# Gates, both projections and the merge of a hybrid decoder block computed with the tokens stationary in the array, and the merged result laid out by feature by way of DRAM

## The chip, the core and the metric

The kernel runs on one core of one Trainium2 chip. The metric is the device time of one execution in microseconds (us). A core has TensorE for matrix products (PE in the rows; PEld is its loading of the stationary operand), VectorE (DVE), ScalarE (ACT), GpSimd (POOL) and SyncE (SP), each with its own instruction queue that it works off in order, and 16 DMA engines that all queues share. Matrix products end in PSUM, of which VectorE and ScalarE take them away.

## The reference, cut to what matters

One decoder block with 256 tokens, a model width of 2048 and float32 throughout. The part that the change touches:

```python
u = rms_norm(h, g_mix[l])
proj = u @ w_in[l]
q, k, v, z, gb, gc, gate_a, gate_c = jnp.split(proj, split_points, axis=-1)
...
y_attn = sliding_window_attention(q, k, v, attn_sinks[l]) @ w_attn_proj[l]   # (256 x 1024) @ (1024 x 2048)
y_conv = short_gated_conv(z, gb, gc, conv_w[l]) @ w_conv_proj[l]             # (256 x 1024) @ (1024 x 2048)
merged = jax.nn.sigmoid(gate_a) * y_attn + jax.nn.sigmoid(gate_c) * y_conv
h = h + merged @ w_mix_out[l]                                               # (256 x 2048) @ (2048 x 2048)
```

gate_a and gate_c are the last two 2048 columns of proj. Cross-attention over 256 memory tokens and a SwiGLU feed-forward with 5632 hidden features follow.

## The kernel before, in words

Every weight matrix is read once from DRAM, in tiles of two times 128 rows by 512 columns (512 KB), issued on SP into five `raw` buffers (line 81). `split` (lines 56 and 57) makes two float32r halves of a tile: ScalarE rounds it to `whi`, VectorE subtracts to get `wlo`; three buffers each. The activations are kept split in the same way, as `X[:, k, 0]` (high) and `X[:, k, 1]` (low), with features on the partitions. A product is high*high + high*low + low*high.

There are two ways to run such a product over a chunk of 512 output columns:

- `gemm_ft` (lines 85 to 111) holds a 128x128 block of the weight in the array and streams tokens. For each block there is a matmul of 512 columns (high weight against high and low tokens, side by side, line 97) and one of 256 columns (low weight against high tokens, line 101). The result has features on the partitions and fills four PSUM banks; ScalarE copies the right half out (line 108) and VectorE adds the left half (line 142). The rest of the work on a result is held back in `pending` and run among the next chunk's weight tiles.
- `gemm_tf` (lines 113 to 139) holds a 128x128 block of tokens in the array and streams 512 columns of the weight: three matmuls of 512 columns (lines 123, 124, 125) for each of two token blocks. The result has tokens on the partitions and fills two PSUM banks.

The order of the work is that of the code, rearranged by a scheduler at build time that places each engine's instructions; `hooks` attach small pieces of work to a weight tile (to the index k0 of its first 128 rows) of a running product. The stages that matter here, all with `gemm_ft` in the kernel before:

- the gates: eight chunks of 512 columns with 16 row tiles each. `evac_g` adds, scales by the norm factor laid along the tokens (`r0[1]`) and applies the sigmoid into `sa` (attention) or `sc` (convolution). The attention itself (scores, probabilities, values) is hooked into these chunks;
- the projections: four times a chunk of w_attn_proj (8 row tiles, `evac_a`) and a chunk of w_conv_proj (8 row tiles, `evac_m`). `evac_m` merges and splits straight into `MG`, which w_mix_out reads. Loads, sums and transposes of the memory tokens are hooked into these chunks (`mem_hooks`: `mst`, `mnat`, `XM`);
- w_mix_out: four chunks with 16 row tiles, `gemm_tf`, residual add into `h` (line 592). Each finished chunk of `h` is laid out by feature by way of DRAM: `bounce` writes it to the DRAM tile `hd` and reads it back in four pieces into `hst` (lines 227 and 232), on SP's queue; `feat` then lets VectorE transpose blocks of 32x32 (line 212).

## Time and profile before

| | us |
|---|---|
| median of 3 runs | 1450.93 |
| lowest and highest of them | 1450.8 and 1451.27 |
| the profiled execution | 1449.95 |
| its span, first to last instruction | 1448.2 |
| granted TensorE clock over the span, of full speed | 0.997 |

The profile is of one execution. Its rows give the span's times from the first instruction on; the profiled execution's own time is 1.75 us above the span. Busy times of PE are modelled at their ends, so distances between starts tell more than durations do.

### The profile page before, as it was taken

What the parts mean: (1) busy time and instruction counts of PE and PEld (TensorE: products, weight loads), DVE (VectorE), ACT (ScalarE), POOL (GpSimd) and SP (SyncE); (2) the same over time, 40 slices, a digit from 0 to 9 for tenths busy, and PEclk for the clock granted to TensorE, in tenths of its full rate; (3) what the DMA queues carried; (4) which work ended last, traced back from release to release, by engine and by line L of the source; (5) the groups of instructions that cost most, each with busy time, mean ns of one, the idle gap of its engine ahead of it and who ended that gap; (6) DMA issues with size and microseconds to landing.
All of it is one profiled execution on the core that took longest, in us unless ns stands there. A gap on an engine that the chain in (4) does not pass through costs nothing.

```text
span 1448.2 us, 20203 instructions
## 1 busy us (share of the span) xinstructions
PE 1431.6 (99%) x7712; PEld 1224.4 (85%) x7712; DVE 882.8 (61%) x1297; ACT 721.2 (50%) x1111; POOL 61.6 (4%) x90
## 2 busy tenths in 40 slices
PE   8999999999999999999999999999999999999997
PEld 7888888888888888899888888888888888888886
DVE  5458678565569875675665665655444556656554
ACT  6443645555456654556654544544333445445443
POOL 1081000010001000000000000000000000000000
PEclk9999999999999999999999999999999999999999
DMA  8655455576667677755666666666556666666663
GB/s 264 189 176 173 140 167 150 156 222 195 190 200 212 207 257 240 240 191 161 192 186 190 189 189 190 180 199 193 196 190 191 187 191 189 189 190 186 199 195 118
DMA packets 146496, 277.21 MB, mean 191 GB/s; under 512 B 9204, under 2 KB 18000, under 8 KB 146272
## 3 DMA queue, kind: packets, MB, share of 16 engines
q1 hardware_dynamic: 144192, 269.52, 60.9%
q0 software_dynamic: 2176, 6.40, 1.7%
q8 instruction: 60, 0.98, 0.3%
q14 instruction: 36, 0.29, 0.1%
q10 hardware_dynamic: 32, 0.01, 0.0%
HBM read 271.70 MB, written 4.19 MB: 191 GB/s over the span
## 4 chain that ended last, share of the span: by engine, by line
PE 95%; POOL 2%; DMA 1%; issue 1%; DVE 0%; ACT 0%; SPq 0%; ACTq 0%; POOLq 0%; DVEq 0%
PE acc L97 42%; PE acc L101 21%; PE acc L124 10%; PE acc L123 10%; PE acc L125 10%; PE sps L434 1%; PE ops L487 1%; DMA raw<-in_w_in 0%; PE tp L476 0%; POOL sa L339 0%; DMA hst<-hd 0%; DMA hd<-h 0%; POOL sa L342 0%; POOL sa L341 0%; POOL sa L340 0%
## 5 line engine op out<-in xcount | busy, mean ns | idle before, releaser
L57 DVE TENSOR_TENSOR wlo<-raw,whi 128x1024 fp32r<-128x1024 f32 (+1 forms) x506 | 608.3, 1207 | 522.3 <-ACT whi L56 522.1
L56 ACT CAST whi<-raw 128x1024 fp32r<-128x1024 f32 (+1 forms) x506 | 519.4, 1031 | 624.0 <-PE acc L97 353.4
L97 PE MATMUL acc<-X,whi 128*128 128x512 f32 x2368 | 805.0, 395 | 0.0
L101 PE MATMUL acc<-X,wlo 128*128 128x256 f32 x2368 | 607.3, 280 | 0.0
L97 PEld LDWEIGHTS acc<-X,whi 128*128 128x128 f32 x2368 | 435.3, 188 | 83.7 <-issue 0.8
L101 PEld LDWEIGHTS acc<-X,wlo 128*128 128x128 f32 x2368 | 445.5, 188 | 23.8 <-issue 0.8
L125 PE MATMUL acc<-whi,gT 128*128 128x512 f32 x352 | 136.9, 389 | 0.0
L124 PE MATMUL acc<-wlo,gT 128*128 128x512 f32 x352 | 136.9, 389 | 0.0
L123 PE MATMUL acc<-whi,gT 128*128 128x512 f32 x352 | 123.8, 389 | 0.0
L108 ACT COPY half<-acc 128x256 f32<-128x256 f32 x184 | 67.1, 369 | 22.4 <-PE acc L101 20.8
L123 PEld LDWEIGHTS acc<-whi,gT 128*128 128x128 f32 x352 | 66.1, 188 | 13.7
L125 PEld LDWEIGHTS acc<-whi,gT 128*128 128x128 f32 x352 | 66.0, 188 | 13.7
L124 PEld LDWEIGHTS acc<-wlo,gT 128*128 128x128 f32 x352 | 66.1, 188 | 13.7
L124 PE MATMUL acc<-wlo,MG 128*128 128x512 f32 x128 | 49.9, 390 | 0.4 <-DVE wlo L57 0.4
L125 PE MATMUL acc<-whi,MG 128*128 128x512 f32 x128 | 49.8, 389 | 0.0
L198 POOL TENSOR_TENSOR rstd<-ms,mhalf 128x2 f32<-128x2 f32 (+1 forms) x6 | 4.9, 810 | 947.2 <-DVE ms L196 947.2
L123 PE MATMUL acc<-whi,MG 128*128 128x512 f32 x128 | 44.9, 389 | 0.0
L97 PE MATMUL acc<-yc,whi 128*128 128x512 f32 x128 | 44.2, 397 | 0.2 <-DVE s L142 0.2
L97 PE MATMUL acc<-oT,whi 128*128 128x512 f32 x128 | 43.8, 396 | 0.0
L124 PE MATMUL acc<-wlo,X 128*128 128x512 f32 x96 | 37.6, 397 | 0.0
L123 PE MATMUL acc<-whi,X 128*128 128x512 f32 x96 | 34.6, 399 | 2.5 <-ACT X L221 2.5
L125 PE MATMUL acc<-whi,X 128*128 128x512 f32 x96 | 36.7, 393 | 0.0
(195 smaller groups left out, 1135.7 us busy)
## 6 DMA issues: line engine op xcount, KB each, us to landing
raw<-in_w_ffn_in SPq DMA_DIRECT2D x176, 512.0 KB, 4.4
raw<-in_w_in SPq DMA_DIRECT2D x134, 512.0 KB, 4.4
raw<-in_w_ffn_out SPq DMA_DIRECT2D x88, 512.0 KB, 4.6
raw<-in_w_mix_out SPq DMA_DIRECT2D x32, 512.0 KB, 5.7
raw<-in_w_attn_proj SPq DMA_DIRECT2D x16, 512.0 KB, 4.8
raw<-in_w_conv_proj SPq DMA_DIRECT2D x16, 512.0 KB, 5.1
raw<-in_w_xkv SPq DMA_DIRECT2D x8, 512.0 KB, 4.2
raw<-in_w_xkv SPq DMA_DIRECT2D x16, 256.0 KB, 2.7
```

The lines of the kernel that those rows point to most:

```text
L56: nc.scalar.copy(hi, src)
L57: nc.vector.tensor_tensor(out=lo, in0=src, in1=hi.bitcast(F32), op=ALU.subtract)
L97: nc.tensor.matmul(ps[m], lhsT=hi[:, k, ms], rhs=X[:, kk].rearrange("p s t -> p (s t)"), start=(kk == 0), stop=False,)
L101: nc.tensor.matmul(ps[m][:, :T], lhsT=lo[:, k, ms], rhs=X[:, kk, 0, :], start=False, stop=(kk == kt - 1),)
L108: nc.scalar.copy(t2, ps[m][:, T:])
L123: nc.tensor.matmul(o, lhsT=xh, rhs=hi[:, k, :cols], start=(kk == 0), stop=False)
L124: nc.tensor.matmul(o, lhsT=xh, rhs=lo[:, k, :cols], start=False, stop=False)
L125: nc.tensor.matmul(o, lhsT=xl, rhs=hi[:, k, :cols], start=False, stop=(kk == kt - 1))
L198: nc.gpsimd.tensor_tensor(out=r, in0=ms, in1=mhalf[:, :n], op=ALU.pow)
L434: nc.tensor.matmul(sps[par][:, j].rearrange("p a b -> p (a b)"), lhsT=qT[b:b + 64, hh // 2, t * P:(t + 1) * P], rhs=kT[b:b + 64, sw, kv // ...
L487: nc.tensor.matmul(ops[64 * par:64 * par + 64], lhsT=v_sb[:, kb, vs], rhs=pt[:, t + kb, par::2, :], start=(kb == 0), stop=(kb == t),)
```

## The change

The gates, both projections and the merge now run with `gemm_tf`: their results have tokens on the partitions, like those of w_mix_out. `evac_g` is one sigmoid on ScalarE out of PSUM, with the norm factor as its per-partition scale. `evac_a` is one product out of PSUM, `evac_m` a product out of PSUM and a sum. A finished chunk of the merge, in `sa`, is written to `hd` in DRAM and read back by feature, all on GpSimd's queue: for the first three chunks into the part of `sc` that is used up, for the last into a new tile `mg`. `mg_feat` (hooked to the next w_conv_proj chunk but one product later) and `mg_last` (hooked to row tiles 12 and 14 of w_mix_out's first chunk) let VectorE transpose it and split it into `MG`. w_mix_out's rows are read in the matching order.

```diff
--- before.py
+++ after.py
@@ -50,6 +50,7 @@
     tiny = ctx.enter_context(tc.tile_pool(name="tiny", bufs=4, side="right"))
     acc = ctx.enter_context(tc.tile_pool(name="acc", bufs=5, space=PSUM))
     tps = ctx.enter_context(tc.tile_pool(name="tps", bufs=3, space=PSUM))
+    dp = ctx.enter_context(tc.tile_pool(name="dp", bufs=2, space=bass.MemoryType.DRAM))
 
 
     def split(hi, lo, src):
@@ feat @@
@@ -212,7 +214,11 @@
             i = nc.vector.transpose(xt[:, k, :].rearrange("p (j b) -> p j b", b=Q), v[:, k0 + k, j0:j0 + nj, :])
             if late and not k:
                 tc.keep_in_program_order(i)
-        high_low([xt[:, k, :] for k in range(n)], kx, g, X, slice(j0 * Q, j0 * Q + nt))
+        tsl = slice(j0 * Q, j0 * Q + nt)
+        if g is None:
+            split(X[:, kx:kx + n, 0, tsl], X[:, kx:kx + n, 1, tsl], xt)
+        else:
+            high_low([xt[:, k, :] for k in range(n)], kx, g, X, tsl)
 
     def high_low(srcs, kx, g, X, tsl=slice(0, T)):
         for k, src in enumerate(srcs):
@@ -226,13 +232,18 @@
         v = src.rearrange("(j b) (i f) -> i b j f", b=Q, i=P // Q)
         eng.dma_start(stage[Q * i:Q * (i + 1), j0:j0 + nj, :], v[i][:, j0:j0 + nj, :])
 
-    def bounce(c, st, eng=nc.sync):
-
+    def bounce_out(src, eng):
         hd = dp.tile([T, C], F32, tag="hd", name="hd")
-        eng.dma_start(hd.rearrange("(t p) f -> p t f", p=P), h[:, :, c * C:(c + 1) * C])
+        eng.dma_start(hd.rearrange("(t p) f -> p t f", p=P), src)
+        return hd
+
+    def bounce_in(hd, st, eng):
         for i in range(P // Q):
             stage_in(st, hd, i, eng=eng)
 
+    def bounce(src, st, eng=nc.sync):
+
+        bounce_in(bounce_out(src, eng), st, eng)
     def spread(r, name):
 
         rB = const.tile([P, T], F32, tag="rB", name=name, bufs=2)
@@ rotary's scratch @@
-        sa = mp.tile([P, KD, T], F32, tag="sa", name="sa")
+        sa = mp.tile([P, D // C, NT, C], F32, tag="sa", name="sa")
 
 
         def rotary(s_sb, nh):
@@ -492,7 +503,7 @@
                 sl = slice(t * P, (t + 1) * P)
                 split(oT[:, 2 * g:2 * g + 2, 0, sl], oT[:, 2 * g:2 * g + 2, 1, sl], ops)
 
-        sc = mp.tile([P, KD, T], F32, tag="sc", name="sc")
+        sc = mp.tile([P, D // C, NT, C], F32, tag="sc", name="sc")
         steps = {
             0: [qk_T], 1: [lambda: scores(0)], 2: [lambda: probs_T(0), lambda: scores(1)],
             3: [lambda: values(0), lambda: probs_T(1), lambda: scores(2)],
@@ -540,33 +551,26 @@
                     hooks = {0: [lambda: do["stage"](0)], 2: [lambda: do["stage"](1)],
                              4: [lambda: do["nat"](0)], 6: [lambda: do["nat"](1)]}
 
-                def evac_g(m, p0, p1, c=c, dst=dst):
-                    o = dst[:, c * (C // P) + m, :]
-                    add(o, p0, p1)
-                    yield
-                    scale(o, r0[1])
-                    nc.scalar.activation(o, o, AF.Sigmoid)
-
-                gemm_ft(W, KD, X1, base + c * C, evac_g, hooks=hooks)
+                def evac_g(t, p, c=c, dst=dst):
+                    nc.scalar.activation(dst[:, c, t, :], p, AF.Sigmoid, scale=r0[0][:, t:t + 1])
+
+                gemm_tf(W, KD, X1, base + c * C, evac_g, hooks=hooks)
 
 
         MG = xp.tile([P, KD, 2, T], F32R, tag="X", name="MG")
+        NC4 = C // P
+
+        def mg_feat(c, k):
+            feat(sc[:, c].rearrange("p t (j f) -> p (t j) f", f=P), NC4, k, 2, c * NC4 + k, None, MG, late=True)
+
         for c in range(D // C):
-            def evac_a(m, p0, p1, c=c):
-                mm = c * (C // P) + m
-                s = sp.tile([P, T], F32, tag="s1", name="s1", bufs=4)
-                add(s, p0, p1)
-                yield
-                nc.vector.tensor_tensor(out=sa[:, mm, :], in0=s, in1=sa[:, mm, :], op=ALU.mult)
-
-            def evac_m(m, p0, p1, c=c):
-                mm = c * (C // P) + m
-                s = sp.tile([P, T], F32, tag="s1", name="s1", bufs=4)
-                add(s, p0, p1)
-                yield
-                nc.vector.tensor_tensor(out=s, in0=s, in1=sc[:, mm, :], op=ALU.mult)
-                nc.vector.tensor_tensor(out=s, in0=s, in1=sa[:, mm, :], op=ALU.add)
-                split(MG[:, mm, 0, :], MG[:, mm, 1, :], s)
+            def evac_a(t, p, c=c):
+                nc.vector.tensor_tensor(out=sa[:, c, t, :], in0=p, in1=sa[:, c, t, :], op=ALU.mult)
+
+            def evac_m(t, p, c=c):
+                o = sc[:, c, t, :]
+                nc.vector.tensor_tensor(out=o, in0=p, in1=o, op=ALU.mult)
+                nc.vector.tensor_tensor(out=sa[:, c, t, :], in0=o, in1=sa[:, c, t, :], op=ALU.add)
 
             def mem_hooks(g):
                 hk = {2: [lambda: do["sums"](g)], 4: []}
@@ -577,12 +581,16 @@
                     hk[4].append(lambda: do["turn"](g, 2))
                     if g < 2:
                         hk[4].append(lambda: do["stage"](g + 2))
+                if g % 2 and g > 1:
+                    hk[4].append(lambda: mg_feat(g // 2 - 1, 0))
+                    hk[6] = [lambda: mg_feat(g // 2 - 1, 2)]
                 return hk
 
-            gemm_ft(rows_kp(a["w_attn_proj"][0]), AW // P, oT, c * C, evac_a, hooks=mem_hooks(2 * c))
-            gemm_ft(rows_kp(a["w_conv_proj"][0]), KC, yc, c * C, evac_m, hooks=mem_hooks(2 * c + 1))
-        while pending:
-            next(pending.pop(0), None)
+            gemm_tf(rows_kp(a["w_attn_proj"][0]), AW // P, oT, c * C, evac_a, hooks=mem_hooks(2 * c))
+            gemm_tf(rows_kp(a["w_conv_proj"][0]), KC, yc, c * C, evac_m, hooks=mem_hooks(2 * c + 1))
+            hd = bounce_out(sa[:, c], nc.gpsimd)
+            if c < D // C - 1:
+                bounce_in(hd, sc[:, c].rearrange("p t (j f) -> p (t j) f", f=P), nc.gpsimd)
         ms.close()
 
     def residual(c, ss, r=None):
@@ -597,7 +605,6 @@
         return evac
 
     hp = ctx.enter_context(tc.tile_pool(name="hp", bufs=1, side="right"))
-    dp = ctx.enter_context(tc.tile_pool(name="dp", bufs=2, space=bass.MemoryType.DRAM))
     h = hp.tile([P, NT, D], F32, name="h")
 
 
@@ -620,10 +627,19 @@
 
         def h_stage(c):
             hs[c] = cp.tile([P, NJ, P], F32, tag="hst", name="hst", bufs=4)
-            bounce(c, hs[c])
+            bounce(h[:, :, c * C:(c + 1) * C], hs[c])
 
         def h_feat(c, k, g, X):
             feat(hs[c], C // P, k, 2, c * (C // P) + k, g, X)
+
+        mg = []
+
+        def mg_in():
+            mg.append(cp.tile([P, NJ, P], F32, tag="hst", name="mg", bufs=4))
+            bounce_in(hd, mg[0], nc.gpsimd)
+
+        def mg_last(k):
+            feat(mg[0], NC4, k, 2, (D // C - 1) * NC4 + k, None, MG, late=True)
 
         for c in range(D // C):
             hooks = {4: [lambda: nc.gpsimd.dma_start(h[:, :, c * C:(c + 1) * C], xv[:, :, c * C:(c + 1) * C])]}
@@ -631,7 +647,10 @@
                 hooks[4].append(lambda: h_stage(c - 1))
             if c == D // C - 1:
                 hooks[4].append(mem_rms)
-            gemm_tf(rows_kp(a["w_mix_out"][0]), KD, MG, c * C, residual(c, ss1), hooks=hooks)
+            if not c:
+                hooks[0] = [mg_in]
+                hooks.update({12: [lambda: mg_last(0)], 14: [lambda: mg_last(2)]})
+            gemm_tf(rows_pk(a["w_mix_out"][0], NC4), KD, MG, c * C, residual(c, ss1), hooks=hooks)
 
         xkT = cp.tile([P, XH, T], F32, tag="xkT", name="xkT")
         xs = cp.tile([P, NJ * C], F32, tag="xs", name="xs")
```

Where it moves instructions, at three places. Names: `sa`, `sc` the gates and later the merge; `s1` a product's result; `MG` the split merge; `xt` a transposed piece; `raw_`, `whi_` and `wlo_` with a number one weight tile each.

VectorE at the end of the third chunk of w_attn_proj and in the w_conv_proj chunk behind it (`wlo_4932` before and `wlo_4119` and `wlo_4142` after are tiles of that w_conv_proj chunk). Before:

```order
L57 TENSOR_TENSOR wlo_4715<-raw_4712,whi_4714 128x1024
L142 TENSOR_TENSOR s1_4655<-acc_4532,half_4653 128x256
L560 TENSOR_TENSOR sa_708<-s1_4655,sa_708 128x256
L57 TENSOR_TENSOR wlo_4738<-raw_4735,whi_4737 128x1024
L57 TENSOR_TENSOR wlo_4780<-raw_4777,whi_4779 128x1024
```

After:

```order
L568 TENSOR_TENSOR sa_710<-acc_3989,sa_710 128x512
L568 TENSOR_TENSOR sa_710<-acc_3990,sa_710 128x512
L214 STREAM_TRANSPOSE xt_4111<-sc_1994 128x256 x2
L58 TENSOR_TENSOR wlo_4119<-raw_4116,whi_4118 128x1024
L214 STREAM_TRANSPOSE xt_4134<-sc_1994 128x256 x2
L58 TENSOR_TENSOR MG_3576<-xt_4111,MG_3576 128x2x256
L58 TENSOR_TENSOR wlo_4142<-raw_4139,whi_4141 128x1024
L58 TENSOR_TENSOR MG_3576<-xt_4134,MG_3576 128x2x256
L58 TENSOR_TENSOR wlo_4172<-raw_4169,whi_4171 128x1024
```

The low halves of the last two w_conv_proj tiles (`wlo_4715` and `wlo_4738` before, `wlo_4119` and `wlo_4142` after) now stand behind transposes of the chunk that was merged one product earlier.

VectorE at the start of w_mix_out (before, its tiles 2 to 6 are `wlo_5090` to `wlo_5162`; after, its tiles 2 to 7 are `wlo_4401` to `wlo_4501`). Before:

```order
L57 TENSOR_TENSOR wlo_5090<-raw_5087,whi_5089 128x1024
L568 TENSOR_TENSOR s1_5003<-s1_5003,sa_708 128x256
L142 TENSOR_TENSOR s1_5011<-acc_4902,half_5009 128x256
L568 TENSOR_TENSOR s1_5007<-s1_5007,sa_708 128x256
L57 TENSOR_TENSOR MG_3982<-s1_4999,MG_3982 128x256
L567 TENSOR_TENSOR s1_5011<-s1_5011,sc_1992 128x256
L57 TENSOR_TENSOR MG_3982<-s1_5003,MG_3982 128x256
L568 TENSOR_TENSOR s1_5011<-s1_5011,sa_708 128x256
L57 TENSOR_TENSOR wlo_5108<-raw_5105,whi_5107 128x1024
L57 TENSOR_TENSOR MG_3982<-s1_5007,MG_3982 128x256
L57 TENSOR_TENSOR wlo_5126<-raw_5123,whi_5125 128x1024
L57 TENSOR_TENSOR MG_3982<-s1_5011,MG_3982 128x256
```

After:

```order
L573 TENSOR_TENSOR sa_710<-sc_1994,sa_710 128x512 x2
L58 TENSOR_TENSOR wlo_4401<-raw_4398,whi_4400 128x1024
L58 TENSOR_TENSOR wlo_4419<-raw_4416,whi_4418 128x1024
L58 TENSOR_TENSOR wlo_4437<-raw_4434,whi_4436 128x1024
L58 TENSOR_TENSOR wlo_4455<-raw_4452,whi_4454 128x1024
L214 STREAM_TRANSPOSE xt_4470<-mg_4356 128x256 x2
L58 TENSOR_TENSOR wlo_4478<-raw_4475,whi_4477 128x1024
L214 STREAM_TRANSPOSE xt_4493<-mg_4356 128x256 x2
L58 TENSOR_TENSOR MG_3576<-xt_4470,MG_3576 128x2x256
L58 TENSOR_TENSOR wlo_4501<-raw_4498,whi_4500 128x1024
L58 TENSOR_TENSOR MG_3576<-xt_4493,MG_3576 128x2x256
```

Before, the last of `MG` is written ahead of tile 5; now the last quarter of it comes from `mg`, with tile 6 behind its first transposes and the first split behind tile 6 and the second transposes.

GpSimd's queue from the last-but-one load of memory tokens on. Before:

```order
L524 DMA mnat_4557<-in_mem 128x512
L524 DMA mnat_4685<-in_mem 128x512
L198 TENSOR_TENSOR rstd_5571<-ms_5569,mhalf_87 128x2
L629 DMA h_5036<-in_x 128x2x512 x4
L198 TENSOR_TENSOR rstd_6301<-ms_6299,mhalf_87 128x2
```

After:

```order
L237 DMA hd_3983<-sa_710 128x2x512
L233 DMA sc_1994<-hd_3983 32x8x128 x4
L535 DMA mnat_4091<-in_mem 128x512
L237 DMA hd_4161<-sa_710 128x2x512
L233 DMA sc_1994<-hd_4161 32x8x128 x4
L199 TENSOR_TENSOR rstd_4892<-ms_4890,mhalf_89 128x2
L237 DMA hd_4335<-sa_710 128x2x512
L233 DMA mg_4356<-hd_4335 32x8x128 x4
L645 DMA h_4342<-in_x 128x2x512 x4
```

Each write to `hd` and the four reads of it stand in this queue with the memory loads; the load of `h` comes behind the reads into `mg`.

## Rows read from the trace of the kernel before

**Rows 1.** The page: busy times, and the chain that ended last by engine.

```profile
PE 1431.6 (99%) x7712; PEld 1224.4 (85%) x7712; DVE 882.8 (61%) x1297; ACT 721.2 (50%) x1111; POOL 61.6 (4%) x90
...
PE 95%; POOL 2%; DMA 1%; issue 1%; DVE 0%; ACT 0%; SPq 0%; ACTq 0%; POOLq 0%; DVEq 0%
```

**Rows 2.** Busy times by stretch: gates, projections, w_mix_out.

```profile
core 0: us, PE busy (x) PEld busy (x) DVE busy (x) ACT busy (x) POOL busy (x), PEclk, DMA share, GB/s
248.00:426.50 178.50, 178.50 (x1021) 152.74 (x1020) 101.89 (x144) 92.10 (x150) 6.38 (x11) 1.00 0.64 191
426.50:518.70 92.20, 91.22 (x516) 78.91 (x515) 80.96 (x155) 58.85 (x108) 8.20 (x14) 1.00 0.69 210
518.70:606.40 87.70, 87.32 (x386) 71.94 (x385) 49.59 (x58) 39.51 (x50) 2.93 (x4) 1.00 0.80 255
```

**Rows 3.** The chain that ended last: the same place in two gate chunks, four apart (start, us).

```profile
320.90 0.92 PE acc L97 x4
...
410.04 0.92 PE acc L97 x4
```

**Rows 4.** Timeline of PE: w_ffn_out's first half, 576 matmuls, and what follows.

```profile
976.40 0.39 PE L123 MATMUL acc<-whi,gT 128*128 128x512 f32 x1
...
1106.98 0.84 PE L97 MATMUL acc<-X,whi 128*128 128x512 f32 x3
```

**Rows 5.** The projections: two shorter stretches, then PE's gaps within them.

```profile
449.00:460.00 11.00, 11.00 (x63) 9.38 (x63) 11.00 (x24) 7.77 (x16) 0.56 (x1) 1.00 0.64 197
460.00:472.00 12.00, 11.02 (x61) 9.11 (x61) 10.90 (x22) 7.08 (x13) 0.55 (x1) 1.00 0.57 192
...
461.37 0.40 PE L97 MATMUL acc<-yc,whi 128*128 128x512 f32 x1
462.53 0.39 PE L101 MATMUL acc<-yc,wlo 128*128 128x256 f32 x1 [0.76 <-DVE wlo L57]
```

**Rows 6.** Groups by line and shape: busy us, mean ns, idle before.

```profile
L57 DVE TENSOR_TENSOR wlo<-raw,whi 128x1024 fp32r<-128x1024 f32 x486 | 594.5, 1229 | 508.9 <-ACT whi L56 508.8
L108 ACT COPY half<-acc 128x256 f32<-128x256 f32 x184 | 67.1, 369 | 22.4 <-PE acc L101 20.8 <-DVE s L142 0.2
L142 DVE TENSOR_TENSOR s<-acc,half 128x256 f32<-128x256 f32 x84 | 32.4, 419 | 1.6 <-ACT half L108 1.6
L592 DVE TENSOR_TENSOR h<-acc,h 128x512 f32<-128x512 f32 x16 | 10.4, 684 | 2.5 <-PE acc L125 2.5
L212 DVE STREAM_TRANSPOSE xt<-mst 128x256 f32<-128x256 f32 x16 | 9.7, 625 | 1.2 <-DMA mst<-in_mem 1.2
L762 DVE TENSOR_TENSOR h<-h,gf 128x512 f32<-128x512 f32 x6 | 3.9, 685 | 0.0
L301 ACT ACTIVATE q_sb<-acc,rstd 128x512 f32<-128x512 f32 x4 | 2.6, 688 | 2.9 <-PE acc L125 2.9
```

**Rows 7.** Timelines of VectorE and SP: the first bounce of h by way of DRAM.

```profile
540.10 1.28 DVE L592 TENSOR_TENSOR h<-acc,h 128x512 f32<-128x512 f32 x2
...
551.65 2.19 DVE L212 STREAM_TRANSPOSE xt<-hst 128x256 f32<-128x256 f32 x4 [3.30 <-DMA hst<-hd]
...
541.45 0.37 SPq L232 DMA_DIRECT2D hd<-h  x1
...
545.67 1.82 SPq L227 DMA_DIRECT2D hst<-hd  x4
```

**Rows 8.** DMA issues in short stretches: KB each, us from issue to landing.

```profile
h<-in_x POOLq DMA_DIRECT2D x1, 512.0 KB, 5.2
...
hd<-h SPq DMA_DIRECT2D x1, 512.0 KB, 6.2
...
mst<-in_mem POOLq DMA_DIRECT2D x4, 128.0 KB, 5.3
```

**Rows 9.** GpSimd's timeline, and landings of all mst loads.

```profile
427.06 2.34 POOL L227 DMA_DIRECT2D mst<-in_mem  x4 [3.42 <-DVE xt L212]
...
DMA to landing us min/median/max: 2.8/5.4/8.2
```

More of the change, by code (lines that the diff above doesn't have):

```diff
@@ L336, in rotary @@
                 sn = rope[:, t:t + 1, 1, :].broadcast_to([P, n8, HD // 2])
-                tm = [sa[:, i, :].rearrange("p (h d) -> p h d", d=HD // 2)[:, :n8, :] for i in range(4)]
+                tm = [sa[:, i // 2, 0, (i % 2) * T:(i % 2 + 1) * T].rearrange("p (h d) -> p h d", d=HD // 2)[:, :n8, :] for i in range(4)]
                 tt = nc.gpsimd.tensor_tensor
```

## The prediction, as written before the changed kernel ran

> **What bounds the kernel now.** The page first: PE is busy for 99% of the span and makes up 95% of the chain of work that ended last [rows 1]. So the time is the sum of what PE streams, and any other engine counts only where PE has to wait for it. By stretches the same holds: in the gates, the projections and w_mix_out PE is busy throughout at a granted clock of 1.00, but for 0.98 us in the projections [rows 2].
>
> Then the price of the two forms of a product. The same place in two gate chunks lies 410.04 - 320.90 = 89.14 us apart, four chunks of `gemm_ft` [rows 3]: 22.285 us for a chunk with 16 row tiles, or 348 ns for a pair of a 512 and a 256 column matmul (64 pairs). The first half of w_ffn_out, `gemm_tf`, takes 1106.98 - 976.40 = 130.58 us for 576 matmuls of 512 columns [rows 4]: 226.7 ns each, 21.76 us for the 96 of a chunk with 16 row tiles. Both forms stream 3072 columns for a row tile and chunk; in the old one that takes eight matmuls, in the new one six, and a column costs a little less.
>
> In the projections the other engines do come in. That stretch takes 92.2 us [rows 2], where four times 22.285 would be 89.1: some 3.1 us too many. Where VectorE has no idle time (11.00 of 11 us, then 10.90 of 12), PE stops, the longest time for a `wlo` that VectorE delivers late [rows 5].
>
> **The change part by part.** *The gates:* eight chunks, each 22.285 - 21.76 = 0.52 us shorter: 4.2 us. VectorE's eight adds and scalings of a chunk (0.42 us each by the row of the add) go, and ScalarE's four copies and four sigmoids become two sigmoids out of PSUM at about 0.69 us, by the one like it for q [rows 6]. Neither engine was PE's limit there, so this is worth nothing by itself.
>
> *The projections:* eight chunks of half the depth, 4 x 0.52 = 2.1 us by the form. VectorE's work on results falls from 24 operations of 0.42 us (10.1 us for a pair of chunks) to four products out of PSUM or sums at 0.68 us each plus two more of them (4.1 us in all, six operations), and for laying out four transposes at 0.62 us and two subtractions at 0.68 us (3.9 us) [rows 6]. Hence 8.0 instead of 10.1 us, and for the first pair, with the memory's transposes beside it, 4.1. I take it that most of the 3.1 us goes too: what stays is 0.25 us, an allowance for two small transposes of the memory's norm factor that PE does in either kernel, and 0.5 us, another for the second pair, where memory work and the first `mg_feat` meet. So 92.2 becomes 4 x 21.76 + 0.75 = 87.8 us: 4.4 us, the 2.1 among them. Bounds of what goes beyond the form: nothing, or all 3.1.
>
> Gain so far: 4.2 + 4.4 = 8.6 us.
>
> *The bounce of the merge:* this is new, and it is on the path where PE needs `MG` or a `wlo` queued behind it. Let e be the time from PE's last matmul of a w_conv_proj chunk to the landing of the merged chunk laid by feature. First the merge: the first token block's product is done as PE ends, then one product and two sums of 0.68 us and the way out of PSUM, 2.4 us [rows 6]. Then GpSimd's issue, for which I allow 0.4 us. Then the write of 512 KB: no row shows a store from GpSimd; a load of the same size there took 5.2 us, SP's stores of h to `hd` 4.2 (the second read of that store's landing is where the reads were issued, 541.45 to 545.67) and 6.2 us [rows 7, 8]; I take 5.0, nearest to the load. Then four reads of 128 KB, issued over 2.34 us in all, so that the last starts 1.75 us after the first [rows 9], and land 5.3 us later [rows 8]. Together e = 2.4 + 0.4 + 5.0 + 0.1 + 1.75 + 5.2 = about 14.9 us. From below: the same bounce on SP's queue has its data 551.65 - 541.38 = 10.3 us after the last add to h [rows 7], which gives e = 12.7. From above: the longest landings, 6.2 and 8.2 us [rows 8, 9], and 0.65 us to issue: e = 19.3.
>
> What waits for it. *At w_mix_out* PE comes to row tile pair 6, which needs the last quarter of `MG`, 6 x 2.72 = 16.3 us after its start, and does two matmuls with high halves and one with `wlo` before it asks for the low half of `MG`: 17.0 us. By the order on VectorE that low half stands behind two transposes, the pair's own `wlo` (1.23 us), two more transposes and then itself: e + 1.24 + 1.23 + 1.24 + 0.68 = e + 4.4. So PE waits e - 12.6: 2.3 us at e = 14.9, next to nothing at 12.7, 6.7 at 19.3. *In the second and third pair's w_conv_proj chunk* two `wlo` stand behind the transposes of the chunk before. PE starts that product 10.9 us after the end from which e counts; its third tile is wanted at 16.8 us and its `wlo` is done at e + 2.5, its fourth at 19.5 and e + 5.6. The second of these is the tighter: PE waits e - 13.9, that is 1.0 us at e = 14.9, 5.4 at 19.3, twice. In the first of the three the scheduler put the transposes behind the chunk's last `wlo`, which VectorE cannot make before some 15.9 us (the buffer comes free with that product's first tile, at 10.9 + 2.7, and the two halves take over 1 us each), so nothing is added there up to e of about 18. Together 2.3 + 2 x 1.0 = 4.3 us.
>
> *The rest.* The load of h is queued behind the reads into `mg`; it then starts at about 11 us into w_mix_out and needs 5.2 us for its first quarter [rows 8], wanted at 21.8: covered by 5 us. The bounce of h itself is as before. The 4 MB more that the DMA engines move lie in stretches where they are busy for 0.69 and 0.80 of the time [rows 2]; the weights are asked for five buffers ahead, so I cost that at nothing; if it isn't so it shows as a longer e.
>
> Sum: 1449.95 (the profiled execution) - 8.6 + 4.3 = 1445.65. The median of the runs stands 0.98 us above that execution, so **1446.6 us**.
>
> On the form of the product the Trainium skill speaks against the change ("TensorE: Matmul & The Clock Gate", section "Back-to-back issue gap"): an isolated matmul of N columns follows the last after N/2.4 + 2.5 ns. By that the old form would take 1300 ns and the new one 1295 ns for a row tile and chunk, and the 192 of them that change would give 1.0 us, an estimate from that page, where the rows give 6.3. The rows here have 348 ns for the pair and 226.7 for the single one, both above the formula, and the pair by more.
>
> **The rivals.** *The bounce is hidden altogether* (0.15): e is 12.7 or less, as SP's bounce would make it; for it speaks that the h bounces, the first one 10.3 us long [rows 7], lie in a stretch where PE is idle for only 0.38 us [rows 2]. All 8.6 us stay: 1442.3. The Trainium skill would have it so ("DMA: Bandwidth & Descriptors", section "Anatomy of one DMA — SWDGE (gpsimd) path"): about 2.0 us and the bytes at 436 GB/s, an estimate of 3.2 and 2.3 us for these sizes. The rows show 5.2 and 5.3 us in this kernel, beside the weights' loads.
>
> *The bounce is late* (0.08 for slower by over 0.2%): e decides. The waits are (e - 12.6) + 2 (e - 13.9); they eat up the 8.6 us at e = 16.3, and the kernel is slower by 0.2% from e = 17.3 on. At 19.3 they are 17.5 us: 1459.8. The slowest of the mst reads took 8.2 us [rows 9]; against it, half of them took 5.4 or less, and the memory's loads end before the second bounce.
>
> *The form gives nothing* (0.04): the gates' and projections' weights and tokens come from other buffers than w_ffn_out's, and the 6.3 us fail. Against it, w_mix_out with 384 matmuls in 87.3 us busy has the same 227 ns [rows 2]. 1449.95 - 2.3 + 4.3 + 0.98 = 1452.9, within 0.2%.
>
> **How the numbers follow.** What this kernel's runs can tell from no change is about 0.2%, or 2.9 us. Faster by more than that needs e below 15.4 and the form's gain; I give the forecast 0.47 in that part, and the hidden bounce 0.15: 0.62 faster. Between e = 15.4 and 17.3, and with the form giving nothing, it is the same: 0.30. Slower: 0.08. The range goes from the hidden bounce, 1442.3, up to e = 16.7, where the waits are 9.7 us: 1452.0.
>
> **What would show it.** A gate chunk of 21.8 us in the chain; the projections' stretch at 88 us apart from waits; VectorE's `xt` waiting for DMA once in each of the last two w_conv_proj chunks and once some 10 us into w_mix_out, and PE waiting for `wlo` or `MG` behind it, 1 us, 1 us and 2 us; `hd` landing about 5 us after its issue. Wrong would make it: landings near 8 us, PE waiting for a gate's PSUM or for the sigmoids, or a pitch over 230 ns in the gates.

## The result and the profile after

| | before | after |
|---|---|---|
| median, us | 1450.87 (1450.31 to 1451.27) | 1461.42 (1458.79 to 1462.47) |
| ratio, 95% interval | | 1.0069 [1.0056, 1.0082] |
| profiled execution, its span | 1449.95, 1448.2 | 1461.56, 1459.8 |

The changed kernel is slower by 0.7%. The forecast, 1446.6 us and faster, was wrong, and the time lies outside its range.

The page of the profile after, against [rows 1]: busy times, and the chain that ended last by engine.

```profile
PE 1435.3 (98%) x7328; PEld 1210.5 (83%) x7328; DVE 857.0 (59%) x1185; ACT 699.0 (48%) x1023; POOL 73.8 (5%) x110
...
PE 62%; DMA 1%; issue 1%; POOL 0%; DVE 0%; ACT 0%; ACTq 0%; POOLq 0%; DVEq 0%
```

The chain is followed back from the end, and here it ends at 528.9 us, in GpSimd's queue at the last bounce. It says nothing of the three bounces before, and its 62% is no measure of what PE lost.

The stretches of the changed kernel: gates, projections, w_mix_out (columns as in [rows 2]).

```profile
246.00:423.70 177.70, 177.70 (x787) 142.68 (x787) 85.66 (x93) 83.48 (x108) 6.41 (x11) 1.00 0.66 192
423.70:525.00 101.30, 94.57 (x389) 75.42 (x388) 72.94 (x103) 47.12 (x67) 17.53 (x29) 0.95 0.78 219
525.00:618.20 93.20, 89.90 (x385) 73.42 (x384) 50.80 (x54) 38.55 (x46) 5.93 (x9) 0.96 0.82 254
```

The gates are full, and end earlier: at 423.7 instead of 426.5. The loss is in the other two stretches: 101.3 us against 92.2, and 93.2 against 87.7. There PE is idle for 6.7 and 3.3 us, and the mean granted clock is 0.95 and 0.96 instead of 1.00. Both have one origin. First VectorE's timeline: the transposes that read the four bounces, with the wait before each in brackets, and the `wlo` behind the first of them; then PE's: the first matmul after each of its stops.

```profile
468.12 2.18 DVE L214 STREAM_TRANSPOSE xt<-sc 128x256 f32<-128x256 f32 x4 [5.61 <-DMA sc<-hd]
470.22 1.19 DVE L58 TENSOR_TENSOR wlo<-raw,whi 128x1024 fp32r<-128x1024 f32 x1
...
491.29 1.14 DVE L214 STREAM_TRANSPOSE xt<-sc 128x256 f32<-128x256 f32 x2 [6.54 <-DMA sc<-hd]
517.16 1.16 DVE L214 STREAM_TRANSPOSE xt<-sc 128x256 f32<-128x256 f32 x2 [3.49 <-DMA sc<-hd]
542.63 1.14 DVE L214 STREAM_TRANSPOSE xt<-mg 128x256 f32<-128x256 f32 x2 [7.24 <-DMA mg<-hd]
...
471.46 0.73 PE L125 MATMUL acc<-wlo,oT 128*128 128x512 f32 x1 [2.52 <-DVE wlo L58]
493.59 0.79 PE L125 MATMUL acc<-wlo,yc 128*128 128x512 f32 x1 [3.52 <-DVE wlo L58]
519.48 0.50 PE L125 MATMUL acc<-wlo,yc 128*128 128x512 f32 x1 [0.70 <-DVE wlo L58]
544.48 1.22 PE L124 MATMUL acc<-whi,MG 128*128 128x512 f32 x2 [3.27 <-ACT MG L57]
```

VectorE waits at each bounce for 3.5 to 7.2 us, every `wlo` in its queue waits with it, and PE stops: 10.0 us in all. Then PE's clock, in short stretches behind the second and the last long stop (the tenth column is the granted clock, and the first count is PE's matmuls):

```profile
495.00:497.00 2.00, 2.00 (x6) 1.58 (x5) 2.00 (x4) 1.84 (x4) 0.00 (x0) 0.50 0.70 250
499.00:501.00 2.00, 2.00 (x11) 1.60 (x10) 1.62 (x2) 0.35 (x1) 0.00 (x0) 1.00 0.81 263
...
546.00:548.00 2.00, 1.96 (x5) 1.17 (x4) 2.00 (x3) 1.56 (x2) 0.00 (x0) 0.50 0.84 301
550.00:552.00 2.00, 2.00 (x10) 1.63 (x10) 0.54 (x1) 1.05 (x1) 0.00 (x0) 0.98 0.79 237
```

After each of the three long stops PE runs at 0.50 to 0.55 of full speed, the 1.2 GHz level, for some 3.5, 5.3 and 5.6 us: five or six matmuls in 2 us where the rows at full clock count ten or eleven, those at the edges included. By the starts of its matmuls one takes 427 ns there instead of 227 to 233, so of these 14.4 us about 46%, 6.6 us, are lost. A busy share does not show that: PE counts as busy for all of 495 to 499. Stops and slow clock make 16.6 us.

### The profile page after: what moved, and what is told of

Same layout as the page of the kernel before. It is cut to its first block, busy times and chain, and to the rows that moved or that the text cites. A ratio compares the mean times of both kernels' runs of the same rounds, so it can differ in the third digit from the quotient of the medians.

```text
span 1459.8 us, 19244 instructions
## 1 busy us (share of the span) xinstructions
PE 1435.3 (98%) x7328; PEld 1210.5 (83%) x7328; DVE 857.0 (59%) x1185; ACT 699.0 (48%) x1023; POOL 73.8 (5%) x110
## 4 chain that ended last, share of the span: by engine, by line
PE 62%; DMA 1%; issue 1%; POOL 0%; DVE 0%; ACT 0%; ACTq 0%; POOLq 0%; DVEq 0%
PE acc L98 24%; PE acc L102 12%; PE acc L126 8%; PE acc L124 8%; PE acc L125 8%; DMA mg<-hd 1%; PE tp L742 0%; PE ops L724 0%; PE sps L699 0%; POOL mg L233 0%; PE tp L716 0%; ACTq L862 0%; DVE h L777 0%; DMA hd<-sa 0%; ACT junk L187 0%
## 5 line engine op out<-in xcount | busy, mean ns | idle before, releaser
L98 PE MATMUL acc<-X,whi 128*128 128x512 f32 x1856 | 630.6, 395 | 0.0
L102 PE MATMUL acc<-X,wlo 128*128 128x256 f32 x1856 | 475.9, 280 | 0.0
L98 PEld LDWEIGHTS acc<-X,whi 128*128 128x128 f32 x1856 | 341.2, 188 | 65.1 <-issue 0.8
L102 PEld LDWEIGHTS acc<-X,wlo 128*128 128x128 f32 x1856 | 349.3, 188 | 18.5 <-DVE wlo L58 0.7
L125 PE MATMUL acc<-wlo,X 128*128 128x512 f32 x352 | 138.1, 394 | 0.0
L126 PE MATMUL acc<-whi,X 128*128 128x512 f32 x352 | 137.1, 393 | 0.0
L124 PE MATMUL acc<-whi,X 128*128 128x512 f32 x352 | 125.4, 393 | 1.9 <-ACT X L227 1.9
L124 PEld LDWEIGHTS acc<-whi,X 128*128 128x128 f32 x352 | 66.0, 189 | 16.6 <-ACT X L227 2.3
L125 PEld LDWEIGHTS acc<-wlo,X 128*128 128x128 f32 x352 | 66.3, 188 | 15.7 <-issue 1.2
L126 PEld LDWEIGHTS acc<-whi,X 128*128 128x128 f32 x352 | 66.5, 189 | 13.6
L109 ACT COPY half<-acc 128x256 f32<-128x256 f32 x120 | 44.0, 370 | 14.4 <-PE acc L102 14.0
L126 PE MATMUL acc<-whi,MG 128*128 128x512 f32 x128 | 50.5, 397 | 0.0
```

The lines of the kernel that those rows point to most:

```text
L98: nc.tensor.matmul(ps[m], lhsT=hi[:, k, ms], rhs=X[:, kk].rearrange("p s t -> p (s t)"), start=(kk == 0), stop=False,)
L102: nc.tensor.matmul(ps[m][:, :T], lhsT=lo[:, k, ms], rhs=X[:, kk, 0, :], start=False, stop=(kk == kt - 1),)
L109: nc.scalar.copy(t2, ps[m][:, T:])
L124: nc.tensor.matmul(o, lhsT=xh, rhs=hi[:, k, :cols], start=(kk == 0), stop=False)
L125: nc.tensor.matmul(o, lhsT=xh, rhs=lo[:, k, :cols], start=False, stop=False)
L126: nc.tensor.matmul(o, lhsT=xl, rhs=hi[:, k, :cols], start=False, stop=(kk == kt - 1))
```

## The experiments

The median of the kernel before, on the chips of these runs, was 1450.9 to 1452.1 us, and ratios are to the runs of the same chip. MG, `sa`, `sc` and `hd` are as in the change.

**The wait, or the transfers?** First, all transfers as in the change, but no one waits for them (`mg_last` likewise, out of XM):

```diff
-            feat(sc[:, c].rearrange(...), NC4, k, 2, c * NC4 + k, None, MG, late=True)
+            feat(sa[:, c].rearrange(...), NC4, k, 2, c * NC4 + k, None, MG, late=True)
```

> The changed kernel with its bounce issued as it is, but with transposes that read data which is already there (the merge itself for three quarters, memory features for the last), so that nothing waits for the bounce; MG then holds the wrong layout. If the waits for the bounce and TensorE's slow clock behind them are the whole loss (my theory: 18.5 us of gaps in the trace), this takes 1461.4 - 18.5 = about 1443 us. If it is the traffic of the bounce that delays the weights, it stays near 1455 to 1461. If the new form of the products is itself slow, it stays above 1451.

Second, without `bounce_out`, `bounce_in` and `mg_in` as well.

> As the kernel with the bounce issued and not waited for, but without the bounce's DMAs at all (four writes of 512 KB and sixteen reads of 128 KB are left out; MG holds the wrong layout). Theory of the waits: the same time within 1.5 us, about 1442 us. Theory of the traffic: clearly faster than the kernel that still issues them, by 5 us or more.

Measured: 1446.06 us, 0.9959 [0.9944, 0.9974], and 1444.84 us, 0.9954 [0.9939, 0.9969]. So the transfers cost 1 us or nothing, and waiting for them costs 15.4 us by the medians (about 16 by the two ratios, as the chips differ). Without waits the change is worth 6.0 us against the kernel before on the same chip. Neither came down to 1443: the gain is smaller than I had it, too.

The first run shows the bounces undisturbed. GpSimd's timeline: the four stores into `hd`, and the reads behind each; then, bounce by bounce, the time from issue to landing of its four reads (into `sc`, `sc`, `sc` and `mg`).

```profile
453.55 0.74 POOL L237 DMA_DIRECT2D hd<-sa  x1 [8.60 <-DVE sa L573]
...
458.30 2.33 POOL L233 DMA_DIRECT2D sc<-hd  x4 [2.19 <-DMA hd<-sa]
...
472.50 0.72 POOL L237 DMA_DIRECT2D hd<-sa  x1 [4.61 <-DVE sa L573]
477.94 2.36 POOL L233 DMA_DIRECT2D sc<-hd  x4 [4.73 <-DMA hd<-sa]
...
494.81 0.72 POOL L237 DMA_DIRECT2D hd<-sa  x1 [13.94 <-DVE sa L573]
498.65 2.36 POOL L233 DMA_DIRECT2D sc<-hd  x4 [3.12 <-DMA hd<-sa]
...
517.35 0.76 POOL L237 DMA_DIRECT2D hd<-sa  x1 [15.59 <-DVE sa L573]
521.95 2.34 POOL L233 DMA_DIRECT2D mg<-hd  x4 [3.84 <-issue]
...
DMA to landing us min/median/max: 7.0/9.2/9.8
DMA to landing us min/median/max: 5.5/7.0/7.2
DMA to landing us min/median/max: 6.8/7.0/8.0
DMA to landing us min/median/max: 3.4/5.3/6.7
```

PE's last matmuls of these chunks start at 447.5, 469.8, 492.1 and 514.7. The first store is issued 6 us after that, since VectorE has `wlo` and the memory's work between the four operations of the merge; the other three 2.7 us after. The reads go out 4.8, 5.4, 3.8 and 4.6 us behind the stores (I had 5.0). The last of the four is issued 1.75 us later and lands after 9.8, 7.2, 8.0 and 6.7 us (I had 5.2). So e, from those matmuls to the last landing, is 22.4, 17.1, 16.3 and 15.8 us. On the reads the Trainium skill ("DMA: Bandwidth & Descriptors", section "Anatomy of one DMA — SWDGE (gpsimd) path") does not agree with the trace: 2.0 us and the bytes at 436 GB/s give 2.3 us, an estimate from that page, where the fastest of the sixteen took 3.4 us and the median into `sc` is 7.1.

**SP's queue instead of GpSimd's** (`nc.gpsimd` becomes `nc.sync` in all calls of the bounce).

> The changed kernel with all DMAs of the merge's bounce on SP's queue in place of GpSimd's. If GpSimd's queue makes the bounce long, reads land 3 to 4 us sooner (4.0 us as for hst before, against 6.5 to 9.1 now), the three long stops of TensorE shrink below 1 us, the clock stays up, and the time is about 1445 us. If the pieces are slow because of what else the DMA engines do, landings stay at 6 to 9 us and the time at 1456 to 1462.

1455.16 us, 1.0028 [1.0018, 1.0037]: 6 us better than the change, no more. The reads into `sc` land in 5.0 us (median), those of the first bounce in 8.0 to 8.7; VectorE still waits for the first three chunks 5.4, 7.1 and 2.9 us, and PE stops for 3.5 and 2.4 us before a `wlo`.

**No DRAM at all.** TensorE turns the 32 blocks of 128 by 128, and w_mix_out's rows have the old order.

```diff
+            tp = tps.tile([P, 2, T], F32, tag="tp", name="tp")
+            for i in range(2):
+                for t in range(NT):
+                    nc.tensor.transpose(tp[:, i, t * P:(t + 1) * P], sa[:, c, t, (k + i) * P:(k + i + 1) * P], ident)
+            kx = c * NC4 + k
+            split(MG[:, kx:kx + 2, 0, :], MG[:, kx:kx + 2, 1, :], tp)
...
```

> The new products and the merge with results by token as in the change, but MG is made by 32 transposes of 128x128 on TensorE (about 0.11 us each by the rows of the feed-forward's own transposes, 3.5 us in all) and no bounce, w_mix_out's rows in the old order. Theory of the waits: 1443 + 3.5 = about 1446 us, faster than before by 4 to 5 us. If products by token are no gain: 1451 or more.

1449.37 us, 0.9982 [0.9973, 0.9992]: no stop of PE, clock 1.00, and 3.3 us above the run without waits, 0.1 us for each transpose. In its gates the first sigmoids of two chunks start at 359.20 and 380.96, 21.76 us apart, exactly the price I had.

**What a stop costs.** In the kernel that turns on TensorE, six single long sums on VectorE among the gates' splittings:

```diff
+            tc.keep_in_program_order(nc.vector.tensor_reduce(
+                idle[:, :n], sa[:, 0, 0:1, :].broadcast_to([P, n, C]), axis=AX.X, op=ALU.add))
...
```

> The kernel that turns the merge on TensorE (1449.4 us, no stop), with six single sums on VectorE put between its wlo in the gates; they take about 4.8, 5.9, 6.9, 8.0, 9.6 and 12.3 us (512 columns times 9 to 23 at VectorE's 0.53 us each), and their results go nowhere. VectorE is some 4 us ahead there, so TensorE should stop for about 0.6, 1.7, 2.7, 3.8, 5.4 and 8.1 us, 22 us in all. Theory (a stop of some 2.5 us or more costs a second time, by 3.5 to 5.5 us at the granted clock of about 0.5): after the two short stops the pitch stays at 227 ns, after the four long ones it is 427 ns for 3 to 6 us, which adds 1.6 to 2.8 us each: 1449 + 22 + 9 = 1480 us. Rival (the half clock in the change belongs to the DMA engines' load or to the projections, not to the stop): the pitch is 227 ns right after every stop, 1471 us.

1472.69 us, one execution: near the rival's number, 1471, though not by its reason. The third to fifth sum (VectorE), the stop that each makes (PE), and the clock right behind the stop:

```profile
355.08 7.08 DVE L519 TENSOR_REDUCE idle<-sa 128x13 f32<-128x6656 f32 x1
372.52 8.15 DVE L519 TENSOR_REDUCE idle<-sa 128x15 f32<-128x7680 f32 x1
397.55 9.75 DVE L519 TENSOR_REDUCE idle<-sa 128x18 f32<-128x9216 f32 x1
...
363.35 0.74 PE L125 MATMUL acc<-wlo,X 128*128 128x512 f32 x1 [1.91 <-DVE wlo L58]
381.85 0.50 PE L125 MATMUL acc<-wlo,X 128*128 128x512 f32 x1 [2.98 <-DVE wlo L58]
408.49 0.80 PE L125 MATMUL acc<-wlo,X 128*128 128x512 f32 x1 [4.58 <-DVE wlo L58]
...
363.40:366.00 2.60, 2.60 (x6) 2.06 (x7) 2.17 (x2) 0.00 (x0) 0.00 (x0) 0.51 0.57 145
381.90:384.00 2.10, 2.10 (x9) 1.75 (x10) 2.10 (x2) 0.00 (x0) 0.00 (x0) 1.00 0.46 80
408.50:413.00 4.50, 4.50 (x11) 3.55 (x12) 2.20 (x2) 0.00 (x0) 0.00 (x0) 0.50 0.75 244
```

The stop is the hold less 5.2 us each time (7.08 and 1.91, 8.15 and 2.98, 9.75 and 4.58): that far ahead is VectorE in the gates. The half clock does follow stops, in a stretch with no bounce. But it came after 1.91, 4.58 and 5.83 us and not after 0.85 or 2.98: length alone does not decide it, and what else does stays open. The stops, 16.8 us in all (the shortest sum makes none), and the slow clock make the 23 us over that kernel's 1449.4.

**Each wait by itself.** The change with some of the transposes reading the merge where it lies, as in the first run: all but the first chunk wait; the first alone; the last alone.

> As the change, but the transposes of the first chunk read the merge where it lies, not what the first bounce brings, so that quarter of MG has another layout; all transfers stay, and the transposes of the other three chunks wait for theirs. Cascade theory (the first chunk's lateness holds up VectorE, the second merge behind it, and so the second chunk): no stop after the first product, the second one's stop falls under 2 us, and no half clock follows it; the stop at w_mix_out stays, 1446 + 6 = about 1452 us. Rival (each bounce is late by itself): the stops at the second chunk and at w_mix_out stay as they are, 3.5 and 3.3 us each with 5 us at half clock, and only the first one's 2.5 us with 1.8 us for the clock goes: about 1457 us.

> The counterpart of the run in which all but the first wait: only the transposes of the first chunk read what the bounce brings; the other three quarters of MG are read where the merge lies, in another layout. All transfers stay. Additive theory (each wait costs by itself): what is missing between the change, 1461.4 us, and that run, 1455.6 us, so 5.8 us over the kernel without waits: 1452 us, one stop of 2 to 3 us in the third w_attn_proj product with some 3 us of half clock behind it. Cascade theory (a late first chunk makes the later ones late, which alone are late by little): no later stop here, for nothing waits, and so less than 3 us, 1449 us.

> Only the transposes of the last chunk, in w_mix_out, read what their bounce brings; the first three quarters of MG are read where the merge lies, in another layout. All transfers stay. My prediction's term for this place, 2.3 us and no price for the clock: 1446.1 + 2.3 = 1448.4 us. Corrected theory (by the kernel without waits the last chunk lands some 15 to 17 us after its matmuls, so a stop of 2.4 to 4.4 us, and some 2.5 us more at half clock when the stop is over 2 us): 1450 to 1452 us. Cascade theory (this bounce is late only because the ones before it are): under 1448 us, no stop over 1 us before the last quarter.

Measured 1455.61 us (1450.46 to 1461.26), 1449.99 and 1448.51. Over the 1446.06 without waits that is 9.5, 3.9 and 2.4 us. First and the rest make 13.4 of the 15.4, so the waits mostly add up. The 2 us left are not clear of the spread of these runs; that one wait delays the next does show in the change, where the second store, at 476.4, goes out 8.4 us after its matmuls instead of 2.7. The cascade as the main cause is out, as the rest is late without the first. The last alone costs about what I had for that place (2.3 us): stops of 1.52 and 0.90 us, no half clock. That is luck in part: its data were there after 16.3 us, for which my e - 12.6 gives 3.7.

**Later transposes, first try.** One product later, and two; the last chunk, or the last two, turned on TensorE (`mg_turn`, with the lines above).

```diff
-                if g % 2 and g > 1:
+                late = {4: 0, 6: 1, 7: 2}
+                if g in late:
...
```

> The chunks of the first two bounces are transposed one product later than in the change (in the third and fourth w_attn_proj product, over 30 us after the matmuls that end them, where the slowest path took 23 us); the third stays where it is, and the last chunk is turned by eight transposes on TensorE, with no bounce. Nothing is left out. Theory (the loss is VectorE's wait for a late chunk, which stops TensorE, and the lower clock after a long stop): no stop of 2 us or more, at most one under 1 us in the last w_conv_proj chunk, granted clock 1.00 in both stretches; 1446 us of the kernel that waits for nothing, and 1 us for eight transposes: 1447 us (1446 to 1449). Rival (the stores and reads through DRAM slow the weights' loads wherever the transposes stand): stops of 2 to 4 us stay, 1452 us or more.

> The first two chunks still go through DRAM, but are transposed two products later than in the change (in the third and fourth w_conv_proj product; the chunks' own matmuls end three products ahead); the third and fourth chunk are turned by sixteen transposes on TensorE. Nothing is left out. Theory (the bounce takes 18 to 23 us from the last matmul of its chunk, not 15, and VectorE works some 5 us ahead of TensorE; one product later was too little, two are enough): no stop over 1 us, granted clock 1.00, 1446.1 us of the kernel without waits and some 0.1 us for each of sixteen transposes: 1447.5 us (1446 to 1449). Rival (VectorE itself is too full in these products, wherever the transposes stand): stops of 1 to 2 us stay, 1452 us.

1453.01 us, 1.002 [1.001, 1.003], and 1449.56 us, 0.9989 [0.9979, 0.9999]. Both missed, for a reason that VectorE's timelines give: the first chunk's transposes in the one and the other.

```profile
466.53 0.64 DVE L214 STREAM_TRANSPOSE xt<-sc 128x256 f32<-128x256 f32 x1 [3.57 <-DMA sc<-hd]
...
471.89 0.63 DVE L214 STREAM_TRANSPOSE xt<-sc 128x256 f32<-128x256 f32 x1 [5.72 <-DMA sc<-hd]
```

The projections start at 424.15 and 427.36 there, and at 423.69 in the change. In all three the wait begins 38.8 us behind that. The scheduler had put the transpose, which no call held in place, where it stood before; the runs tell nothing on the delay.

**Second try: the order held fast.** All transposes and all splittings of the projections are kept in program order; and the same with the last chunk's bounce.

> As the run with transposes one product later, but now they really stand there: in that run and in the one with two products the scheduler had put the first chunk's transposes on VectorE where they stood in the change (the wait for them began 38.8 us into the projections in all three), so neither had tested the delay. Here the splittings into wlo in the projections are kept in program order, and all transposes with them: the first chunk's stand in the third w_conv_proj to fourth w_attn_proj products' work by program order (one product later), the second's likewise, the third's behind the last wlo of the projections, and the last chunk is turned by eight transposes on TensorE. Nothing is left out. Theory (the wait is the loss; with 11 us more the bounce of 16 to 23 us is covered): no wait of VectorE for a bounce over 1 us, no half clock, 1446.1 us and some 0.8 us for eight transposes: 1447 us (1446 to 1448.5). Rival (VectorE is too full in these products, so that TensorE stops for wlo wherever the transposes stand): 1449.5 us or more, as with the run meant to be two products later.

> As the run before, but the last chunk too goes by way of DRAM, as in the change. Nothing is left out. Theory: what the run in which only the last chunk waits has over the run without waits, 2.4 us: 1448.5 us (1447.5 to 1450), with stops in w_mix_out alone. Rival (the last bounce is later here, or a half clock follows its stop): 1451 us or more.

1468.07 us, 1.0118 [1.0098, 1.0137], and 1472.08 us, 1.014 [1.0122, 1.0158]. In the first VectorE waits for no bounce, but a product's first `wlo` may no longer be made ahead of the merge before it, and PE stops for 1.4 to 2.9 us at the start of every product but the first. A fault of the experiment; what it shows is how much that lead is worth.

**Third try.** A chunk's transposes are kept behind the merge of the next chunk, and the splittings left free; then the same with the last bounce as in the change.

```diff
-            if late and not k:
+            if late:
...
-                nc.vector.tensor_tensor(out=o, in0=p, in1=o, op=ALU.mult)
+                tc.keep_in_program_order(nc.vector.tensor_tensor(out=o, in0=p, in1=o, op=ALU.mult))
...
+            if c:
+                mg_feat(c - 1, 0)
+                mg_feat(c - 1, 2)
```

> The delay once more, without the fault of the two pinned runs, in which the order kept VectorE from splitting the next product's first weights ahead of a merge (TensorE stopped at each product's start, and nothing waited for a bounce). Here the transposes of a chunk are kept behind the merge of the next one, some 22 us after the matmuls of their own, and the splittings are left free. The last chunk is turned by eight transposes on TensorE. Nothing is left out. Theory (the wait is the loss, and later transposes take it away): VectorE waits for no bounce or for under 1 us, TensorE stops for no wlo over 1.3 us, no half clock; 1446.1 us of the kernel without waits and 0.8 us for eight transposes: 1447 us (1446 to 1448.5). Rival (VectorE is too full around the merges): stops of over 1 us at the products' starts, 1450 us or more.

> As the run before, with the last chunk too by way of DRAM, as in the change: all that the change does, with the first three chunks' transposes later by half a product to one and a half. Nothing is left out. Theory: 2.4 us for the last chunk's wait, as measured alone: 1448.5 us (1447.5 to 1450). Rival (a longer stop there, with half clock behind it, as in the change): 1451 us or more.

1446.24 us, 0.9968 [0.9957, 0.9979], faster than both kernels; and 1451.26 us, 1.0002 [0.9993, 1.0011], where 1448.5 was expected. The page's chain by engine, and VectorE's first two waiting places, of the first:

```profile
PE 95%; POOL 2%; DMA 1%; issue 0%; DVE 0%; SPq 0%; ACT 0%; ACTq 0%; POOLq 0%
...
473.04 1.15 DVE L214 STREAM_TRANSPOSE xt<-sc 128x256 f32<-128x256 f32 x2
475.81 1.17 DVE L214 STREAM_TRANSPOSE xt<-sc 128x256 f32<-128x256 f32 x2
```

No bracket: the data are there. Three bounces are now hidden and cost nothing that can be measured. The fourth, whose data w_mix_out's first chunk needs some 16 us after their matmuls, takes the whole gain back; an order of w_mix_out that needs them later was not tried. In the second kernel, whose profiled execution took 1453.58 us and is one of the slowest of ten, VectorE's wait, PE's stop and the clock behind it:

```profile
534.67 2.17 DVE L214 STREAM_TRANSPOSE xt<-mg 128x256 f32<-128x256 f32 x4 [6.68 <-DMA mg<-hd]
...
536.51 0.80 PE L124 MATMUL acc<-whi,MG 128*128 128x512 f32 x1 [5.47 <-ACT MG L57]
...
538.50:540.50 2.00, 1.98 (x6) 1.53 (x6) 1.79 (x3) 0.00 (x0) 0.00 (x0) 0.50 0.73 215
```

The store went out at 517.99, 3.5 us after PE came to w_mix_out; the reads left 6.0 us behind it, and their median landing was 7.6. The last bounce alone (2.4 us, above) was not so late. Its price was 2.4 us in that pair of kernels and is 5.0 in this; what makes the difference was not tested.

**Why a matmul of the projections is slower.** In the run without waits they take 89.5 us for 384 matmuls, 233 ns each, where gates and w_ffn_out [rows 4] have 227. First, VectorE filled with short operations in three gate chunks; then three gate chunks with other tokens, or in two halves:

> The kernel that turns the merge on TensorE, with VectorE filled in three gate chunks, three or four short operations before each wlo: additions of 128 by 256 in the fourth gate chunk, transposes of 128 by 128 in the fifth, scalings of 128 by 256 in the sixth; VectorE is then busy for about 0.9 there instead of 0.45. Their results go nowhere. What is asked: in the projections a matmul of 512 columns takes 232 to 233 ns, with or without the bounce, against 226.7 ns in the gates and w_ffn_out. Theory (a VectorE busy nearly throughout, 0.8 to 0.9, slows the matmuls beside it): 231 to 234 ns in one or more of the filled chunks, 22.3 us a chunk instead of 21.76, 0.5 to 1.6 us more in all. Rival (the pitch belongs to the projections' own operands or depth): 226 to 227 ns in all three, time within 0.3 us of 1449.4.

```diff
-                gemm_tf(W, KD, X1, base + c * C, evac_g, hooks=hooks)
...
+                    gemm_tf(W, KD, {4: yc, 7: oT}.get(i - 1, X1), base + c * C, evac_g, hooks=hooks)
```

> The kernel that turns the merge on TensorE, with three gate chunks changed, which makes these gates wrong: the fifth takes yc for the tokens, the eighth oT, and the sixth is made as two products of half the depth. As many matmuls as before in each. What is asked: why a 512 column matmul takes 232.5 ns in the projections and 226.7 ns in the gates, when a full VectorE does not slow it. Theory A (it goes with the tiles oT and yc as the stationary operand): 232 ns in the fifth and eighth chunk, 227 in the sixth. Theory B (with the depth of eight row tiles): 232 ns in the sixth alone. Rival C (with neither; something else that runs in that stretch): 227 ns in all three.

1449.45 and 1452.38 us. One execution each. Filled, a chunk still takes 21.76 us (with transposes: first sigmoids at 337.71 and 359.47), with VectorE busy for 18.14 of 21.7 us. Of the second run, ScalarE's first sigmoid behind the fourth to eighth gate chunk:

```profile
339.58 0.69 ACT L556 ACTIVATE sa<-acc,rstd 128x512 f32<-128x512 f32 x1 [0.54 <-PE acc L127]
361.87 0.69 ACT L556 ACTIVATE sc<-acc,rstd 128x512 f32<-128x512 f32 x1 [0.58 <-PE acc L127]
383.69 0.69 ACT L556 ACTIVATE sc<-acc,rstd 128x512 f32<-128x512 f32 x1 [0.54 <-PE acc L127]
405.45 0.69 ACT L556 ACTIVATE sc<-acc,rstd 128x512 f32<-128x512 f32 x1 [0.54 <-PE acc L127]
427.88 0.67 ACT L556 ACTIVATE sc<-acc,rstd 128x512 f32<-128x512 f32 x1
```

With `yc` 22.29 us, in halves 21.82, as it was 21.76, with `oT` 22.43 (with X1 that last chunk takes 21.94, from 402.72 to 424.66 in the kernel that turns on TensorE). So the tile that holds the tokens makes it, some 5 ns a matmul. Why these tiles are slower than X1, MG or gT was not tried.

## Why the prediction was wrong, step by step

*The form of the product.* The price was right: 21.76 us a chunk. The last four gate chunks, without attention's matmuls between theirs, take 422.93 - 335.71 = 87.2 us up to the last's first sigmoid, 21.8 each. The gates as a whole gained 3.1 of the 4.2 us: from the same transposes of attention (234.95 before, 235.13 after) to the first matmul of the projections it is 191.65 and 188.56 us. The missing 1.1 us lies in the first four, among attention's matmuls; it was not looked into.

*"I take it that most of the 3.1 us goes too"*: it stays. I laid the projections' excess to VectorE, next to whose full stretches PE had stopped [rows 5]. Only those 0.98 us were VectorE's. More than half of the rest is in the matmuls with `oT` or `yc`: some 5 ns in each of the new form, and as much in a pair of the old one (353 ns by the median distance of starts, where four gate chunks give 348). No relief of VectorE can bring that back. The stretch came to 89.5 us without waits, not 87.8. That is 1.7 us less, and with the gates 2.8 less than my 8.6; measured without waits, the gain is 6.0.

*e = 14.9 us* is the term that failed: 22.4, 17.1, 16.3 and 15.8 us where nothing waits, the first of them above my upper bound of 19.3. The store was right (5.0; 3.8 to 5.4), and so was the merge with its issue (2.8; 2.7) but for the first chunk, beside which VectorE has the memory's work (6.0). The last read was short (5.2; 6.7 to 9.8). The weights are loaded beside all four bounces, and a price of that I had put into a longer e; but no run leaves these loads out, so that they make the reads long is not shown.

*"Nothing is added there up to e of about 18"*, at the first bounce, was no error in itself: in the change the data are there 22.3 us after the matmuls (445.8 to 468.1), PE stops for 2.5 us, and so the place bears 19.8. What was wrong is that I put no price beyond it, not even in the rival with e at 19.3. The transposes stand behind the chunk's last `wlo` but ahead of the first `wlo` of the next product, and PE stops for that one: 2.5 us in the change, and 3.9 us in all with this wait alone.

At the other three places (the two in the projections are those of the third and fourth pair) my formulas with these undisturbed e give 3.2 us in w_mix_out, 3.2 and 2.4 in the projections, 8.8 together; the change's stops there are 3.3, 3.5 and 0.7, or 7.5. So the paths from a late bounce to PE were about right, and the time that I put on them was wrong.

*The clock* is the term that was missing. I priced a wait at its length; three of the four were followed by 3.5 to 5.6 us at 1.2 GHz, 6.6 us in all. So the late bounce, my rival at 0.08, is what happened: the stops alone, 10.0 us against a gain of 6.0, would have made the kernel slower, and with the clock they make 16.6 us by the trace. Of the 14.8 us between the forecast and the result, 2.6 are missing gain, 5.7 are stops (10.0 for 4.3) and 6.6 the clock; that these make 14.9 is closer than the spread of the runs.

## What to carry to other kernels

A late transfer is paid by everything queued behind the first instruction that waits for it, the next product's work included, so look for the first `wlo` behind the wait, not only for the data's own consumer. Take the transfer's time from the busiest stretch that it runs in: the first bounce took 22.4 us, the last 15.8. Give the wait a place where the data are surely there (here behind the next merge: 1446.2 instead of 1461.4 us, with the last chunk turned on TensorE), and check in the trace that the scheduler left it there. A stop of TensorE can cost nearly twice its length.

## What had not been expected of the hardware

- Half clock behind a stop in the middle of a full stream: after stops of 1.91, 2.52, 3.27, 3.52, 4.58, 5.47 and 5.83 us, but not after 0.85 or 2.98, nor, in the first kernel with the order held fast, after 2.90 or 2.80. In the second of these two kernels it did follow a stop of 2.80 us, at 484.0 (granted clock 0.50 from 485 to 488): length alone does not tell.
- TensorE takes 232 to 233 ns for 512 columns with the tiles `oT` and `yc`, 227 with others; a VectorE busy for 0.84 of the time beside it changes nothing.
- Reads of 128 KB into `sc` from GpSimd's queue took 7.1 us (median, 5.5 to 9.8) beside the weights' loads; on SP's queue 5.0 (2.7 to 8.7).
